# Turning the activations of an encoder trunk by VectorE squares and a trip through memory instead of by TensorE

## The chip, the cores and the metric

The kernel runs on one core of a Trainium2 chip. The metric is the device time of one execution in microseconds (us). TensorE (PE in the rows) does the matrix products; each product is a weight load (PEld) and a matmul that streams up to 512 columns past the loaded weights. ScalarE (ACT) and VectorE (DVE) prepare operands and work on results, GpSimd (POOL) does small statistics, and SyncE (SP) issues every transfer, each in the order of its queue. Each engine works through its own instructions in order.

## The reference, cut to what matters

```python
h = x                                            # (1, 256, 2048) float32
for i in range(2):
    hn = rms_norm(h, attn_norm[i])
    mix = windowed_gqa_sink(hn, ...) if i == 0 else diff_attention(hn, ...)
    h = h + mix                                  # both end in  o @ w_o  (2048 x 2048)
    gu = rms_norm(h, ffn_norm[i]) @ w_ffn_in[i]  # 2048 x 11264
    h = h + (silu(gu[..., :D_FF]) * gu[..., D_FF:]) @ w_ffn_out[i]   # 5632 x 2048
    gate = sigmoid(rms_norm(h, ple_gate_norm[i]) @ ple_w_gate[i])    # 2048 x 2048
    h = h + rms_norm(p[i] @ ple_w_proj[i], ple_post_norm[i]) * gate
```

There are 256 tokens, so every weight is read once from memory (425 MB) and used for two tiles of 128 tokens.

## The kernel before

**Products.** Every weight matrix is cut into groups (`Group`): one strip of 512 output columns, and n blocks ("k-tiles") of 128 input rows. A k-tile of the activations, transposed, is the weight operand of TensorE (`xt`, 128 inputs x 256 tokens), and the 512 columns of the weight matrix stream past it (`ws`). Both are float32 and are split in a high and a low part, so each k-tile costs three matmuls for each of the two token tiles m: x high by w high, x low by w high, x high by w low. That is six matmuls a k-tile (`Group.tile`, L176), 9600 in all.

**Weights.** SyncE loads blocks of four k-tiles into `raw` (two DMAs of 512 KB, three blocks deep, L130). `split_block` turns two k-tiles into one `ws` tile: ScalarE copies the high part (L138), VectorE subtracts it for the low part (L139). I call two k-tiles, twelve matmuls, a pair. The pool of `ws` has four tiles (`WS_BUFS`), and `Feed.next` keeps four ahead: when TensorE's program takes pair p, the split of pair p+3 is written, into the tile that pair p-1 leaves.

**Activations.** The residual `h` and the feed-forward's hidden tiles have tokens on the partitions and must be transposed to become `xt`. `Norm.turn` (L269) and `turn_hidden` (L751) do this on TensorE: eight 128x128 transposes for 512 columns (four k-tiles, two token tiles) into PSUM, then a split into `xt` on ScalarE and VectorE (L206/L207, with the norm's gain L210/L211).

**Order.** TensorE's order is the program's own. `Flow` keeps a heap of delayed pieces of work with due times in estimated us; after each matmul of a group it issues one instruction of the piece that is due, so transposes and attention are strewn between matmuls. `flow.until` forces pieces when a group needs an `xt` that isn't written yet. ScalarE, VectorE and SyncE are ordered by the framework's scheduler.

**Stages.** Attention A: qkv, scores and softmax by head, then the projection in two halves of eight k-tiles over four strips (`project`). Feed-forward: per 512 hidden columns a gate group and an up group of 16 k-tiles (`up` makes `hid`), and after 12, 12, 12 and 8 k-tiles of hidden the output groups (`PARTS`), which add to h. Then the gate of the layer embedding, 16 k-tiles by four strips. Then attention B with qkv strips, projection, and the second feed-forward. Each group that adds the last part of a strip of h calls `Norm.add` for that strip; the next matrix needs the strips in order, four k-tiles each.

Of the kernel before, what the change touches and what calls it, by code (L numbers as in the profile page):

```python
# [12 lines left out]
F32 = mybir.dt.float32  # L13
F32R = mybir.dt.float32r
# [71 lines left out]
def encoder(ctx: ExitStack, tc: tile.TileContext, x, p, attn_norm, ffn_norm, a_w_qkv, a_q_norm,  # L86
# [16 lines left out]
    tiny = pool("tiny", 4)  # L103
    mmp = pool("mmp", 4, bass.MemoryType.PSUM)
    atp = pool("atp", 4, bass.MemoryType.PSUM)

    flow = Flow()

# [33 lines left out]
    class Group:  # L142
# [30 lines left out]
        def tile(self, ps, k, m, ws):  # L173
            x, hi, lo = self.xs[k], ws[:, 0, k % 2, :], ws[:, 1, k % 2, :]
            for i, (a, w) in enumerate(((0, hi), (1, hi), (0, lo))):
                nc.tensor.matmul(ps[m], x[:, a, mslice(m)], w, start=(k == 0 and i == 0),  # L176
                                 stop=(k == self.n - 1 and i == 2))
                flow.tick(MM)

# [34 lines left out]
    def rsqrt(src, n, c, out=None):  # L214
# [10 lines left out]
        nc.gpsimd.tensor_tensor(out=r, in0=y, in1=a, op=ALU.mult)  # L225
        return r

    def gain(c):
        return gains[:, c:c + 1]

    class Stat:
# [18 lines left out]
        def col(self, m):  # L250
            return self.r[:, m:m + 1]

    class Norm:


        def __init__(self, col):
            self.col, self.stat, self.xs = col, Stat(), Slots()

        def add(self, s, delay):
            self.stat.add([h[:, m, s * W:(s + 1) * W] for m in range(NM)])  # L260
            for k in range(s * SK, (s + 1) * SK, 2):
                flow.later(delay, lambda k=k: self.turn(k))

        def turn(self, k):

            ps = at_ps()
            for j in range(2):
                for m in range(NM):
                    nc.tensor.transpose(ps[:, j, mslice(m)], h[:, m, (k + j) * P:(k + j + 1) * P], ident)  # L269
                    yield  # L270
            for j in range(2):
                xt = pair()
                split_scaled(xt[:, 0, :], xt[:, 1, :], ps[:, j, :], gain(self.col + k + j))
                self.xs.put(k + j, xt)

    class Slots:

# [79 lines left out]
                                op0=ALU.subtract, op1=ALU.add)  # L357

    phases = ExitStack()

    def phase(name):

        phases.close()
        return phases.enter_context(tc.tile_pool(name=name, bufs=1, reuse_waits="tile"))


    def qk_norm(srcs, rinv, nh, dh, dup, qp, then):
# [35 lines left out]
                yield  # L403
        split_scaled(dst[:, :, 0, :], dst[:, :, 1, :], ps, g)

    def scores(ps, q, k):

        for m in range(NM):
            for i, (a, b) in enumerate(((0, 1), (1, 0), (0, 0))):
                nc.tensor.matmul(ps[m], q[:, a, mslice(m)], k[:, b], start=(i == 0), stop=(i == 2))  # L410
                yield

    def exps(pss, d, slope, ap, extra=None):

# [42 lines left out]
    class AttentionA:  # L457
        def __init__(self, norm):
            self.norm, self.os, self.kd, self.vp = norm, Slots(), [], []
            self.ap = phase("attn0")  # L460
            self.dist = self.ap.tile([P, NM, T], F32, name="dist")

        def keys_values(self, ps):
# [74 lines left out]
        def weigh(self, j, wts):  # L538
            ps = at_ps()[:, 0, :]
            n = 0  # L540
            for e2 in range(2):
                c0 = j // 4 * P + 64 * (1 - e2)
                for kh in range(2):
                    v, wT = self.vp[kh], wts[e2]
                    for a, b in ((1, 0), (0, 1), (0, 0)):
                        nc.tensor.matmul(ps, v[:, a, c0:c0 + P], wT[:, b, kh, :], start=(n == 0), stop=(n == 11))  # L546
                        n += 1
                        yield
            busy["wT"] -= 2
            o = pair()  # L550
            split(o[:, 0, :], o[:, 1, :], ps)
            self.os.put(j, o)

        def groups(self):
            w, xs = a_w_qkv[0], self.norm.xs
# [3 lines left out]
    class AttentionB:  # L559
# [1 line left out]
            self.os, self.norm, self.hd = Slots(), norm, {}  # L561

        def start(self):
            self.ap = phase("attn1")
            self.dist = self.ap.tile([P, NM, T], F32, name="dist")
            nc.sync.dma_start(out=self.dist, in_=dist_b)

# [10 lines left out]
        def turn_side(self, hd, which, toks, b):  # L578
            s = self.hd.setdefault(hd, {"e": {}})
            t = self.ap.tile([P, 2, 2, T], F32R, name=f"qk{which}", tag=f"qk{which}", bufs=2)  # L580
            yield from to_pairs(t, toks, b * T, (gq_b, gk_b)[which])
            s[which] = t
            if which == 1:
                for c in range(2):
                    flow.later(4.5 + 2.0 * c, lambda c=c: self.scores(hd, c))

        def values(self, s):
            def done(ps):
# [9 lines left out]
        def scores(self, hd, c):  # L598
            s = self.hd[hd]
            flow.until(lambda: 0 in s and 1 in s) if not (0 in s and 1 in s) else None  # L600
            ps = at_ps()
            pss = [ps[:, m, :] for m in range(NM)]
            yield from scores(pss, s[0][:, c], s[1][:, c])
            s["e"][c] = exps(pss, self.dist, 2.0 ** (-8.0 * (hd + 1) / B_H), self.ap)
            if c == 1:
                (e1, r1), (e2, r2) = s["e"][0], s["e"][1]
                r2l = small("r2l")
                nc.vector.tensor_scalar(out=r2l, in0=r2, scalar1=nlam, scalar2=None, op0=ALU.mult)
                for m in range(NM):
                    nc.gpsimd.tensor_scalar(out=e2[:, m, :], in0=e2[:, m, :], scalar1=r2l[:, m:m + 1],  # L610
                                            scalar2=1.0, op0=ALU.mult, op1=ALU.mult)
                    nc.vector.scalar_tensor_tensor(out=e1[:, m, :], in0=e1[:, m, :], scalar=r1[:, m:m + 1],  # L612
                                                   in1=e2[:, m, :], op0=ALU.mult, op1=ALU.add)
                flow.later(9.0, lambda: self.turn(hd, e1))
# [39 lines left out]
        def out(self, hd, on):  # L654
            ps = at_ps()
            for j in range(2):
                for m in range(NM):
                    nc.tensor.transpose(ps[:, j, mslice(m)], on[m][:, j * P:(j + 1) * P], ident)  # L658
                    yield
            for j in range(2):  # L660
                o = pair()
                split_scaled(o[:, 0, :], o[:, 1, :], ps[:, j, :], subln[:, j:j + 1])
                self.os.put(2 * hd + j, o)

        def groups(self):
            w, xs, out = b_w_qkv[0], self.norm.xs, []
# [4 lines left out]
            return out  # L671


    def project(w, os, norm):

        def done(half, s):
            def add(ps):
                add_to_h(ps, s)
                if half == 1:
                    norm.add(s, 3.0)  # L680
            return add
        n = KT // 2

        class Half:
            def __len__(self):
                return max(0, len(os) - n)

            def __getitem__(self, k):
                return os[n + k]
        return [Group(w, half * n * P, n, s, (os, Half())[half], done(half, s))  # L690
                for half in range(2) for s in range(NS)]

    class FeedForward:
        def __init__(self, layer, norm):
# [1 line left out]
            self.pp, self.pstat = [], Stat()  # L696

        def start(self):
            self.fp = fp = phase(f"ffn{self.layer}")
            pt = [fp.tile([P, T], F32, name=f"pt{m}", tag=f"pt{m}", bufs=1) for m in range(NM)]  # L700
            for m in range(NM):
                nc.sync.dma_start(out=pt[m], in_=p[self.layer, 0, mslice(m), :])
            self.post = fp.tile([P, D], F32, name="post")
            nc.sync.dma_start(out=self.post, in_=ple_post_norm[self.layer:self.layer + 1, :].partition_broadcast(P)
                              .rearrange("p o d -> p (o d)"))
            self.pe = fp.tile([P, NM, D], F32, name="pe")
            flow.later(12.0, lambda: self.embedding(pt))

        def embedding(self, pt):
# [5 lines left out]
            for j in range(2):  # L715
                pp = pair()
                split(pp[:, 0, :], pp[:, 1, :], ps[:, j, :])
                self.pp.append(pp)

        def embed(self, s):  # L720
            def done(ps):
# [13 lines left out]
        def up(self, hs, k0):  # L735
            def done(ps):
                hid = []
                for m in range(NM):
# [1 line left out]
                    nc.vector.scalar_tensor_tensor(out=u, in0=ps[m], scalar=self.norm.stat.col(m), in1=self.ss[m],  # L740
                                                   op0=ALU.mult, op1=ALU.mult)
                    hid.append(u)
                for j in range(0, SK, 2):
                    flow.later(2.5, lambda j=j: self.turn_hidden(hid, j, hs, k0 + j))
            return done

        def turn_hidden(self, hid, j0, hs, k0):
            ps = at_ps()
            for j in range(2):
                for m in range(NM):  # L750
                    nc.tensor.transpose(ps[:, j, mslice(m)], hid[m][:, (j0 + j) * P:(j0 + j + 1) * P], ident)  # L751
                    yield
            for j in range(2):
                ht = pair()
                split(ht[:, 0, :], ht[:, 1, :], ps[:, j, :])
                hs.put(k0 + j, ht)

        def out(self, s, last):
            def done(ps):
                add_to_h(ps, s)  # L760
                if last:
                    self.gate.add(s, 3.0)
            return done

        def gated(self, s, nxt):
            def done(ps):
# [7 lines left out]
                    if nxt is None:  # L774
                        nc.sync.dma_start(out=out[mslice(m), c], in_=h[:, m, c])
                if nxt is not None:
                    nxt.add(s, 5.0)
            return done

        def gated_last(self, ps, m):  # L780
# [30 lines left out]

    attn_a = AttentionA(norm_a)
    norm = Norm(C_FFN)
    groups = attn_a.groups() + project(a_w_o[0], attn_a.os, norm)
    norm_b = Norm(C_ATTN + KT)
    groups += FeedForward(0, norm).groups(norm_b)
    attn = AttentionB(norm_b)
    norm = Norm(C_FFN + KT)
    groups += attn.groups() + project(b_w_o[0], attn.os, norm)
    groups += FeedForward(1, norm).groups(None)  # L820
    feed = Feed(groups)

# [85 lines left out]
```

## Time and profile before

| | |
|---|---|
| median of 3 runs | 2377.14 us (2376.62 to 2378.21) |
| the profiled execution, its own time | 2379.22 us |
| its span in the trace | 2377.4 us |
| TensorE busy | 2347.2 us, 99% of the span |
| VectorE, ScalarE busy | 57%, 47% |
| DMA engines | 52% of their time, 428.71 MB moved |

TensorE's busy time says how long something was in its pipeline, not how fast: matmuls overlap one another (a mean of 396 ns each, one started every 227 ns). What a change is worth is read from periods, from one group's start to the next.

### The profile page before, as it was taken

How to read it: one execution, taken by the hardware profiler on the slowest of the kernel's cores; microseconds unless marked ns; L12 is line 12 of the kernel's file. 1: busy time of each engine (PE TensorE's matmuls, PEld its weight loads, DVE VectorE, ACT ScalarE, POOL GpSimd, SP SyncE). 2: the span in 40 equal slices, each digit the busy share in tenths (PEclk: the TensorE clock that was granted, in tenths of full speed). 3: DMA queues.
4: the chain of work that ended last, by engine and by line, in shares of the span. 5: the costliest groups of instructions: out<-in, count | busy, mean ns of one | idle time of the engine just before them, and what ended most of it. 6: DMA issues, size and time to landing. Idle time of an engine off the chain costs nothing.

```text
span 2377.4 us, 28287 instructions
## 1 busy us (share of the span) xinstructions
PE 2347.2 (99%) x10757; PEld 1928.4 (81%) x10757; DVE 1352.4 (57%) x1604; ACT 1121.4 (47%) x1557; POOL 141.4 (6%) x311
## 2 busy tenths in 40 slices
PE   8999999999999999999999999999999999999999
PEld 6877788888888888888878888888888888888887
DVE  5777555555555454566567667655545554455564
ACT  5555454434434434455555554544444434444453
POOL 1342000000000000000110120000000000000000
PEclk9999999999999999999999999999999999999999
DMA  6433455555555555555544545555555555555554
GB/s 236 158 108 106 137 182 191 195 192 189 192 185 190 195 191 191 185 179 193 181 160 162 175 160 179 190 185 185 195 186 195 194 193 183 192 195 195 177 196 141
DMA packets 121569, 428.71 MB, mean 180 GB/s; under 512 B 13552, under 2 KB 16728, under 8 KB 121176
## 3 DMA queue, kind: packets, MB, share of 16 engines
q1 hardware_dynamic: 121432, 426.89, 51.8%
q8 instruction: 84, 1.38, 0.2%
q14 instruction: 53, 0.43, 0.1%
HBM read 424.74 MB, written 2.10 MB: 180 GB/s over the span
## 4 chain that ended last, share of the span: by engine, by line
PE 87%; DVE 1%; ACT 1%; issue 0%; POOL 0%; DVEq 0%; POOLq 0%; ACTq 0%
PE mm L176 84%; PE at L751 1%; PE at L269 1%; PE at L410 1%; PE at L635 1%; DVE ws L139 0%; ACT e L427 0%; PE at L402 0%; DVE e L612 0%; ACT v L210 0%; PE at L441 0%; ACT ws L138 0%; PE at L658 0%; DVE qk L211 0%; POOL e L610 0%
## 5 line engine op out<-in xcount | busy, mean ns | idle before, releaser
L176 PE MATMUL mm<-ws,xt 128*128 128x512 f32 x9600 | 2315.6, 396 | 6.1 <-ACT xt L206 3.9
L176 PEld LDWEIGHTS mm<-ws,xt 128*128 128x128 f32 x9600 | 1792.1, 188 | 404.9 <-ACT xt L206 4.9
L139 DVE TENSOR_TENSOR ws<-raw,ws 128x1024 fp32r<-128x1024 f32 x800 | 978.0, 1224 | 874.2 <-ACT ws L138 873.5
L138 ACT CAST ws<-raw 128x1024 fp32r<-128x1024 f32 x800 | 840.8, 1052 | 1026.8 <-PE mm L176 957.2
L217 POOL TENSOR_SCALAR rs_v<-ssum 128x2 f32<-128x2 f32 x8 | 1.5, 193 | 1707.5 <-DVE ssum L246 1707.5
L298 DVE TENSOR_TENSOR h<-mm,h 128x512 f32<-128x512 f32 x96 | 62.2, 682 | 2.3 <-PE mm L176 2.2
L210 ACT ACTIVATE xt<-at,gains 128x256 fp32r<-128x256 f32 x96 | 44.1, 474 | 32.9 <-DVE xt L211 24.2
L269 PE MATMUL at<-ident,h 128*128 128x128 f32 x192 | 52.4, 287 | 6.2 <-DMA h<-in_x_dram 6.2
L427 ACT ACTIVATE e<-e,nm 128x257 f32<-128x257 f32 (+1 forms) x96 | 48.0, 503 | 21.1 <-DVE nm L424 20.7
L206 ACT CAST xt<-at 128x256 fp32r<-128x256 f32 x108 | 37.9, 372 | 39.9 <-DVE xt L207 31.8
L211 DVE SCALAR_TENSOR_TENSOR xt<-at,gains,xt 128x256 fp32r<-128x256 f32 x96 | 44.7, 480 | 17.8 <-ACT xt L210 17.8
L207 DVE TENSOR_TENSOR xt<-at,xt 128x256 fp32r<-128x256 f32 x108 | 43.3, 418 | 14.0 <-ACT xt L206 14.0
L219 POOL TENSOR_TENSOR rs_y<-rs_v,halves 128x2 f32<-128x2 f32 (+2 forms) x29 | 49.0, 1691 | 2.4
L751 PE MATMUL at<-ident,hid 128*128 128x128 f32 x176 | 47.8, 272 | 0.0
L546 PE MATMUL at<-wT,vp 128*128 128x256 f32 x192 | 45.7, 297 | 1.3 <-DVE wT L207 1.0
L421 DVE SCALAR_TENSOR_TENSOR e<-dist,at 128x256 f32<-128x256 f32 x96 | 36.4, 413 | 10.2 <-PE at L410 9.8
L441 PE MATMUL at<-ident,e 128*128 128x128 f32 x160 | 40.6, 272 | 0.7 <-DVE e L421 0.7
L410 PE MATMUL at<-kd,qT 128*128 128x512 f32 x96 | 36.1, 400 | 3.2 <-DVE wT L207 2.5
L732 ACT ACTIVATE silu<-mm,rinv 128x512 f32<-128x512 f32 x44 | 29.9, 688 | 19.7 <-PE mm L176 19.7
L526 POOL TENSOR_SCALAR e<-e,rd 128x256 f32<-128x256 f32 x64 | 33.0, 532 | 60.4 <-DVE rd L430 60.0
L546 PEld LDWEIGHTS at<-wT,vp 128*128 128x128 f32 x192 | 33.9, 204 | 2.9 <-ACT e L427 1.1
L269 PEld LDWEIGHTS at<-ident,h 128*128 128x128 f32 x192 | 27.7, 147 | 9.4 <-DMA h<-in_x_dram 7.1
(97 smaller groups left out, 671.7 us busy)
## 6 DMA issues: line engine op xcount, KB each, us to landing
raw<-in_w_ffn_in_dram SPq DMA_DIRECT2D x352, 512.0 KB
raw<-in_w_ffn_out_dram SPq DMA_DIRECT2D x176, 512.0 KB
raw<-in_b_w_qkv_dram SPq DMA_DIRECT2D x96, 512.0 KB
raw<-in_ple_w_gate_dram SPq DMA_DIRECT2D x64, 512.0 KB
raw<-in_a_w_qkv_dram SPq DMA_DIRECT2D x40, 512.0 KB
raw<-in_a_w_o_dram SPq DMA_DIRECT2D x32, 512.0 KB
raw<-in_b_w_o_dram SPq DMA_DIRECT2D x32, 512.0 KB
raw<-in_ple_w_proj_dram SPq DMA_DIRECT2D x16, 256.0 KB
```

Source lines behind the costliest of these rows:

```text
L138: nc.scalar.copy(out=ws[:, 0], in_=src)
L139: nc.vector.tensor_tensor(out=ws[:, 1], in0=src, in1=ws[:, 0].bitcast(F32), op=ALU.subtract)
L176: nc.tensor.matmul(ps[m], x[:, a, mslice(m)], w, start=(k == 0 and i == 0), stop=(k == self.n - 1 and i == 2))
L210: nc.scalar.activation(out=hi, in_=src, func=AF.Copy, scale=scale)
L211: nc.vector.scalar_tensor_tensor(out=lo, in0=src, scalar=scale, in1=hi.bitcast(F32), op0=ALU.mult, op1=ALU.subtract)
L219: nc.gpsimd.tensor_tensor(out=y, in0=v, in1=halves[:, :n], op=ALU.pow)
L269: nc.tensor.transpose(ps[:, j, mslice(m)], h[:, m, (k + j) * P:(k + j + 1) * P], ident)
L298: nc.vector.tensor_tensor(out=hs, in0=ps[m], in1=hs, op=ALU.add)
L410: nc.tensor.matmul(ps[m], q[:, a, mslice(m)], k[:, b], start=(i == 0), stop=(i == 2))
L427: nc.scalar.activation(out=sc[:, m, :], in_=sc[:, m, :], func=AF.Exp, bias=nm[:, m:m + 1], accum_out=den[:, m:m + 1])
L546: nc.tensor.matmul(ps, v[:, a, c0:c0 + P], wT[:, b, kh, :], start=(n == 0), stop=(n == 11))
L751: nc.tensor.transpose(ps[:, j, mslice(m)], hid[m][:, (j0 + j) * P:(j0 + j + 1) * P], ident)
```

## The change

Four things change.

1. `Norm.add` and `up` no longer write TensorE transposes but call `turned`. VectorE turns the two 128x512 token tiles in 32x32 squares, with tokens of the two tiles side by side (element step two); SyncE writes the 512 KB to memory, and reads it back in four DMAs whose runs are 64 floats, so that the 128 rows of a k-tile lie on the partitions. The split into `xt` then reads SBUF. The tokens of such an `xt` alternate between the token tiles, so the weight load takes every second element (`alternate`); other `xt` keep halves (`halves_of`).
2. The tiles for the squares and the way back come from pools of the stage: `wT` in attention A, `qk0` and `qk1` in attention B, new ones in the feed-forward.
3. In attention B the six score matmuls of a map stand together, and are due 6.5 us after the keys instead of 4.5.
4. The projection of attention A is cut in parts of 8, 4 and 4 k-tiles instead of 8 and 8.

```diff
+    def halves_of(t):
+        return t.rearrange("p a (m t) -> p a m t", m=NM)
+    def alternate(t):
+        return t.rearrange("p a (t m) -> p a m t", m=NM)
...
-                nc.tensor.matmul(ps[m], x[:, a, mslice(m)], w, start=(k == 0 and i == 0),
+                nc.tensor.matmul(ps[m], x[:, a, m], w, start=(k == 0 and i == 0),
...
+    def turned(srcs, then):
+        (tag0, tag1), ap = spare[0], spare[1]
+        both = [ap.tile([P, 2, 2, T], F32R, name=t, tag=t, bufs=n).bitcast(F32).rearrange("p a b t -> p (a b t)")
+                for t, n in (tag0, tag1)]
+        st = both[0].rearrange("p (f t m) -> p f m t", m=NM, t=32)
+        for m in range(NM):
+            nc.vector.transpose(out=st[:, :, m, :], in_=srcs[m].rearrange("p (f t) -> p f t", t=32))
+        d = dram.tile([P, 2 * W], F32, name="sq32")
+        nc.sync.dma_start(out=d, in_=both[0])
+        def read():
+            for b in range(4):
+                r = slice(32 * b, 32 * b + 32)
+                nc.sync.dma_start(out=both[1][r].rearrange("f (k g i) -> f k g i", k=SK, g=4),
+                                  in_=d.rearrange("(g f) (k b i) -> b f k g i", g=4, k=SK, b=4)[b])
+            flow.later(4.0, lambda: then(both[1].rearrange("f (k t) -> f k t", k=SK)))
+        flow.later(3.0, read)
...
-        def add(self, s, delay):
-            self.stat.add([h[:, m, s * W:(s + 1) * W] for m in range(NM)])
-            for k in range(s * SK, (s + 1) * SK, 2):
-                flow.later(delay, lambda k=k: self.turn(k))
+        def add(self, s):
+            hs = [h[:, m, s * W:(s + 1) * W] for m in range(NM)]
+            self.stat.add(hs)
+            def then(xT):
+                for j in range(SK):
+                    xt, k = pair(), s * SK + j
+                    split_scaled(xt[:, 0, :], xt[:, 1, :], xT[:, j], gain(self.col + k))
+                    self.xs.put(k, alternate(xt))
+            turned(hs, then)
...
-                for j in range(0, SK, 2):
-                    flow.later(2.5, lambda j=j: self.turn_hidden(hid, j, hs, k0 + j))
+                def then(xT):
+                    for j in range(SK):
+                        ht = pair()
+                        split(ht[:, 0, :], ht[:, 1, :], xT[:, j])
+                        hs.put(k0 + j, alternate(ht))
+                turned(hid, then)
...
-                    flow.later(4.5 + 2.0 * c, lambda c=c: self.scores(hd, c))
+                    flow.later(6.5 + 2.0 * c, lambda c=c: self.scores(hd, c))
...
-    groups = attn_a.groups() + project(a_w_o[0], attn_a.os, norm)
+    groups = attn_a.groups() + project(a_w_o[0], attn_a.os, norm, (8, 4, 4))
...
-    groups += attn.groups() + project(b_w_o[0], attn.os, norm)
+    groups += attn.groups() + project(b_w_o[0], attn.os, norm, (8, 8))
```

**ScalarE, the sixth up group of the first feed-forward** (hidden columns 2560 to 3071, the last before the second round of output groups). `CAST ws<-raw` is a weight split, `CAST xt` the high part of a turned hidden tile. Before:

```order
L732 ACTIVATE silu<-mm,rinv 128x512 x2
L138 CAST ws<-raw 128x1024 x10
L206 CAST xt<-at 128x256 x3
L138 CAST ws<-raw 128x1024
L206 CAST xt<-at 128x256
L138 CAST ws<-raw 128x1024 x29
```

Of the change (one silu of the gate group stands between the previous turned tile and these rows):

```order
L207 CAST xt<-turned 128x256 x4
L777 ACTIVATE silu<-mm,rinv 128x512
L139 CAST ws<-raw 128x1024 x14
L207 CAST xt<-turned 128x256 x4
L139 CAST ws<-raw 128x1024 x27
```

The four turned tiles stand four weight splits later than the first of them stood. VectorE's rows run in the same order behind them.

**SyncE, the same place.** `raw` are weight loads, `sq` the tile in memory, `turned` the way back. Before there are weight loads alone. Of the change:

```order
L131 DMA raw<-in_w_ffn_in_dram 128x1024 x6
L131 DMA raw<-in_w_ffn_out_dram 128x1024 x8
L272 DMA sq_5251<-sq_5247 128x1024
L131 DMA raw<-in_w_ffn_out_dram 128x1024 x2
L277 DMA turned<-sq_5251 32x16x64 x4
L131 DMA raw<-in_w_ffn_out_dram 128x1024 x14
```

One block of weights stands between the way out and the way back, and the loads behind wait in the queue for both.

**SyncE, from the projection of attention B to the second feed-forward.** `pt` is the layer embedding's input, 2 x 128 KB, that TensorE transposes early in the feed-forward; `post` its gain. Before:

```order
L130 DMA raw<-in_b_w_o_dram 128x1024 x20
L702 DMA pt_12008<-in_p_dram 128x256
L702 DMA pt_12009<-in_p_dram 128x256
L704 DMA post<-in_ple_post_norm_dram 128x2048
L130 DMA raw<-in_b_w_o_dram 128x1024 x12
L130 DMA raw<-in_w_ffn_in_dram 128x1024 x16
```

Of the change:

```order
L272 DMA sq_12026<-qk_12022 128x1024
L131 DMA raw<-in_w_ffn_in_dram 128x1024 x2
L277 DMA qk_12023<-sq_12026 32x16x64 x4
L131 DMA raw<-in_w_ffn_in_dram 128x1024 x3
L747 DMA pt_12032<-in_p_dram 128x256
L747 DMA pt_12033<-in_p_dram 128x256
L749 DMA post<-in_ple_post_norm_dram 128x2048
```

The loads of `pt` move from ahead of the last twelve loads of the projection to behind the way back of the last strip and three DMAs of weights.

## Rows read from the trace of the kernel before

**Rows 1.** The page's first lines: span, busy time of TensorE
```profile
span 2377.4 us, 28287 instructions
PE 2347.2 (99%) x10757; PEld 1928.4 (81%) x10757; DVE 1352.4 (57%) x1604; ACT 1121.4 (47%) x1557; POOL 141.4 (6%) x311
```

**Rows 2.** The chain of waits, longest pieces: start us, us, what
```profile
354.32 44.48 PE mm L176 x196
...
1078.98 20.00 PE mm L176 x88
1101.74 20.00 PE mm L176 x88
```

**Rows 3.** Groups by line and shape: count | busy us, mean ns | idle before
```profile
L176 PE MATMUL mm<-ws,xt 128*128 128x512 f32 x9600 | 2315.6, 396 | 6.1 <-ACT xt L206 3.9 <-DVE xt L207 1.4 <-DVE ws L139 0.5
L176 PEld LDWEIGHTS mm<-ws,xt 128*128 128x128 f32 x9600 | 1792.1, 188 | 404.9 <-ACT xt L206 4.9 <-DVE xt L207 2.9 <-DVE ws L139 1.5
...
L298 DVE TENSOR_TENSOR h<-mm,h 128x512 f32<-128x512 f32 x96 | 62.2, 682 | 2.3 <-PE mm L176 2.2
L269 PE MATMUL at<-ident,h 128*128 128x128 f32 x192 | 52.4, 287 | 6.2 <-DMA h<-in_x_dram 6.2
L751 PE MATMUL at<-ident,hid 128*128 128x128 f32 x176 | 47.8, 272 | 0.0
```

**Rows 4.** Busy time by window, end of attention A: PE, PEld, DVE, ACT, POOL, PEclk, DMA, GB/s
```profile
248.00:268.00 20.00, 15.18 (x69) 11.71 (x69) 7.16 (x13) 6.36 (x15) 1.88 (x4) 0.83 0.33 119
252.40:258.60 6.20, 5.51 (x15) 4.45 (x16) 0.64 (x2) 0.15 (x1) 0.00 (x0) 0.50 0.89 307
```

**Rows 5.** Who waited for whom, TensorE: us in total, times, longest
```profile
PE at L410 <- DVE qk L211: 5.0, 4, 2.3
```

**Rows 6.** Windows in attention B, columns as in rows 4
```profile
1214.00:1217.00 3.00, 0.73 (x5) 0.31 (x4) 3.00 (x6) 1.39 (x2) 0.00 (x0) 1.00 0.00 0
1218.00:1221.40 3.40, 3.40 (x13) 2.82 (x12) 2.57 (x4) 0.72 (x2) 0.00 (x0) 0.51 0.81 282
1293.00:1296.00 3.00, 2.10 (x11) 1.50 (x10) 2.88 (x4) 1.03 (x2) 0.53 (x2) 1.00 0.99 315
1296.00:1299.40 3.40, 3.40 (x20) 2.95 (x20) 2.57 (x4) 0.67 (x1) 0.00 (x0) 1.00 0.21 43
```

**Rows 7.** Timeline of ScalarE and VectorE, first feed-forward: start, us, instruction, idle before
```profile
764.13 1.05 ACT L138 CAST ws<-raw 128x1024 fp32r<-128x1024 f32 x1 [0.29 <-PE mm L176]
765.08 0.37 ACT L206 CAST xt<-at 128x256 fp32r<-128x256 f32 x1
...
765.21 1.23 DVE L139 TENSOR_TENSOR ws<-raw,ws 128x1024 fp32r<-128x1024 f32 x1 [0.87 <-ACT ws L138]
766.35 0.42 DVE L207 TENSOR_TENSOR xt<-at,xt 128x256 fp32r<-128x256 f32 x1
```

**Rows 8.** Timeline where an up group ends and the next group begins
```profile
348.61 1.40 DVE L740 SCALAR_TENSOR_TENSOR hid<-mm,rinv,silu 128x512 f32<-128x512 f32 x2
348.67 2.89 PE L176 MATMUL mm<-ws,xt 128*128 128x512 f32 x12
```

**Rows 9.** A block of weights: SyncE issues, then windows, columns as in rows 4
```profile
771.93 6.20 SPq L130 DMA_DIRECT2D raw<-in_w_ffn_in_dram  x4
...
772.50:773.00 0.50, 0.50 (x4) 0.41 (x3) 0.00 (x0) 0.50 (x1) 0.00 (x0) 1.00 0.32 66
773.00:776.00 3.00, 3.00 (x15) 2.49 (x14) 1.22 (x1) 1.38 (x2) 0.00 (x0) 1.00 0.95 332
776.00:776.50 0.50, 0.50 (x4) 0.42 (x3) 0.43 (x1) 0.03 (x1) 0.00 (x0) 1.00 0.17 57
```

**Rows 10.** SyncE and TensorE at the start, loads of x in 1 KB runs; issues of two
```profile
1.17 0.93 SPq L324 DMA_DIRECT2D h<-in_x_dram  x2
3.99 2.19 PE L269 MATMUL at<-ident,h 128*128 128x128 f32 x8 [1.17 <-DMA h<-in_x_dram]
...
331.49 0.80 SPq L130 DMA_DIRECT2D raw<-in_ple_w_proj_dram  x2
```

More of the change, by code (lines that the diff above doesn't have):

```diff
@@ L105, in encoder @@
     atp = pool("atp", 4, bass.MemoryType.PSUM)
+    dram = pool("turned", 4, bass.MemoryType.DRAM)
     flow = Flow()
@@ L273, in turn @@
                 split_scaled(xt[:, 0, :], xt[:, 1, :], ps[:, j, :], gain(self.col + k + j))
-                self.xs.put(k + j, xt)
+                self.xs.put(k + j, halves_of(xt))
     class Slots:
@@ L359, in encoder, with phase @@
     phases = ExitStack()
-    def phase(name):
+    spare = [None, None]
+    def phase(name, tags):
         phases.close()
-        return phases.enter_context(tc.tile_pool(name=name, bufs=1, reuse_waits="tile"))
+        spare[:] = tags, phases.enter_context(tc.tile_pool(name=name, bufs=1, reuse_waits="tile"))
+        return spare[1]
     def qk_norm(srcs, rinv, nh, dh, dup, qp, then):
@@ L404, in to_pairs, with scores @@
         split_scaled(dst[:, :, 0, :], dst[:, :, 1, :], ps, g)
-    def scores(ps, q, k):
+    def scores(ps, q, k, together=False):
         for m in range(NM):
@@ L410, in scores @@
                 nc.tensor.matmul(ps[m], q[:, a, mslice(m)], k[:, b], start=(i == 0), stop=(i == 2))
-                yield
+                if not together:
+                    yield
+        if together:
+            yield 0.7
     def exps(pss, d, slope, ap, extra=None):
@@ L551, in weigh @@
             split(o[:, 0, :], o[:, 1, :], ps)
-            self.os.put(j, o)
+            self.os.put(j, halves_of(o))
         def groups(self):
@@ L563, in start @@
         def start(self):
-            self.ap = phase("attn1")
+            self.ap = phase("attn1", (("qk0", 2), ("qk1", 2)))
             self.dist = self.ap.tile([P, NM, T], F32, name="dist")
@@ L602, in scores @@
             pss = [ps[:, m, :] for m in range(NM)]
-            yield from scores(pss, s[0][:, c], s[1][:, c])
+            yield from scores(pss, s[0][:, c], s[1][:, c], True)
             s["e"][c] = exps(pss, self.dist, 2.0 ** (-8.0 * (hd + 1) / B_H), self.ap)
@@ L662, in out @@
                 split_scaled(o[:, 0, :], o[:, 1, :], ps[:, j, :], subln[:, j:j + 1])
-                self.os.put(2 * hd + j, o)
+                self.os.put(2 * hd + j, halves_of(o))
         def groups(self):
@@ L671, in groups, with project, __init__, __len__ @@
             return out
-    def project(w, os, norm):
-        def done(half, s):
+    def project(w, os, norm, parts):
+        class Part:
+            def __init__(self, first):
+                self.first = first
+            def __len__(self):
+                return max(0, len(os) - self.first)
+            def __getitem__(self, k):
+                return os[self.first + k]
+        def done(last, s):
             def add(ps):
                 add_to_h(ps, s)
-                if half == 1:
-                    norm.add(s, 3.0)
-            return add
[L682 to L691, printed above, removed]
+                if last:
+                    norm.add(s)
+            return add
+        out, first = [], 0
+        for n in parts:
+            out += [Group(w, first * P, n, s, Part(first), done(first + n == KT, s)) for s in range(NS)]
+            first += n
+        return out
     class FeedForward:
@@ L698, in start @@
         def start(self):
-            self.fp = fp = phase(f"ffn{self.layer}")
+            self.fp = fp = phase(f"ffn{self.layer}", (("sq32", 2), ("turned", 2)))
             pt = [fp.tile([P, T], F32, name=f"pt{m}", tag=f"pt{m}", bufs=1) for m in range(NM)]
@@ L717, in embedding @@
                 split(pp[:, 0, :], pp[:, 1, :], ps[:, j, :])
-                self.pp.append(pp)
+                self.pp.append(halves_of(pp))
         def embed(self, s):
@@ L742, in done @@
                     hid.append(u)
-                for j in range(0, SK, 2):
-                    flow.later(2.5, lambda j=j: self.turn_hidden(hid, j, hs, k0 + j))
-            return done
[L747 to L756, printed above, removed]
+                def then(xT):
[4 more added lines that the diff above has]
+                turned(hid, then)
+            return done
         def out(self, s, last):
@@ L761, in done @@
                 if last:
-                    self.gate.add(s, 3.0)
+                    self.gate.add(s)
             return done
@@ L776, in done @@
                 if nxt is not None:
-                    nxt.add(s, 5.0)
+                    nxt.add(s)
             return done
```

2 lines of the change are left out of this document (1 added, 1 removed).

## The prediction

> **What bounds the kernel now.** The page first [rows 1]: something is in TensorE's pipeline for 2347 of 2377 us, so a gain comes from taking work off TensorE or from its few waits, and a loss from new waits. Then the groups [rows 3]: 9600 of the 10757 matmuls are the weights' own. How fast these run is read from the chain of waits [rows 2], where an undisturbed piece is 196 matmuls in 44.48 us, 0.2269 us each. 9600 of them are 2179 us, and that part stays. About 200 us are transposes, attention and waits.
>
> **Transposes removed.** Their mean of 272 to 287 ns [rows 3] is latency. Their cost is in the period: between two pieces of the chain that begin alike, at 1078.98 and 1101.74, lie 22.76 us [rows 2], a group of 96 matmuls and the eight transposes strewn into it. 96 x 0.2269 are 21.79. So eight cost 0.97 us, 0.12 each: they slip in beside long matmuls. `turned` is called for 22 hidden tiles and for 20 strips of five norms (the first norm of x keeps its transposes), 42 calls of eight. Gain: 42 x 0.97 = **40.8 us**.
>
> **Projection in three parts.** At the end of attention A the second half needs heads 12 to 15 before they are done. [...] With parts of 8, 4 and 4 the k-tiles 12 to 15 are wanted 96 matmuls (22 us) later, and the strewn attention work has room. Gain: **7.9 us**. The four more groups cost eight VectorE additions of 0.68 us [rows 3], beside TensorE's work.
>
> **Scores together.** Four waits on the split keys are 5.0 us [rows 5]; after the longest (2.27 us) the clock was 0.51 for 3.4 us, 1.7 us lost, while after a wait of 0.9 us it stayed at 1.00 [rows 6]. Due 2 us later, the scores find the keys in three of four cases. [...] I take **4 us** gained, between 0 and 6.7.
>
> Gains: 40.8 + 7.9 + 4 = 52.7 us.
>
> **What the moved work waits for.** A turned tile now goes VectorE, SyncE, memory, SyncE, ScalarE, VectorE. Two delays decide, the queue and the trip.
>
> *The queue.* The split of pair p+3 needs the `ws` tile that pair p-1 leaves. Counting ScalarE's rows of the change, 12 of the 42 turned tiles stand right behind the weight split that waits for the pair just ahead of the one that needs them: hidden tiles 2, 5 and 8 of both feed-forwards, the last strip of both gates and of attention B's norm, and strips 0 to 2 after attention A. So, however early the data lands, TensorE finishes pair p-1, the weight split starts, and only then the tile's. These rows exist already: a split released by TensorE at 764.13, its tile's high part from 765.08, and VectorE's low part done at 766.77, 2.64 us on [rows 7]. TensorE can run one matmul with the high part meanwhile, so each place costs **2.5 us** (2.6 with a gain): 6 x 2.5 + 6 x 2.6 = 30.6 us. In the order before, these splits stood four weight splits earlier, and nothing waits there [rows 3]. For the other tiles the order leaves at least two pairs.
>
> *The trip.* From the end of an up group (348.67) VectorE has `hid` 1.35 us later [rows 8]. The squares: no row has such an operation. Nearest is 0.68 us for 128x512 [rows 3]; between 0 and twice that, I take 0.68 each, done at 2.7. SyncE issues in 0.4 us [rows 10]; after an issue at 771.93 a block of 1 MB begins to move some 0.6 us later and has moved by about 776.1 [rows 9], 3.6 us for 1 MB in all; the half that a pair needs takes about 1.6. The first load of x is 2.8 us from issue to use [rows 10]; its 256 KB at the same rate are 0.8, the start 0.6, and of the 1.4 left I give 0.8 to the issue and 0.6 to landing. So the write lands at 2.7 + 0.6 + 1.6 + 0.6 = 5.5. Meanwhile a block of weights (1 MB) has gone in front of the way back; it ends near 7.6. The way back is 2048 runs of 256 bytes, which no row shows: 1.6 us if like long runs, 6 at near four times that; I take 3, nearer the long runs, which are the nearest row; the factor of four is a guess that only makes the upper end. With 0.6 to land: **11.2 us** after the group's end, between 8 and 16.
>
> The output groups want hidden tile 10, the last of the part of eight k-tiles, after four k-tiles, 5.45 us: 11.2 + 0.8 for the split [rows 7] - 5.45 - 0.23 = **6.3 us** wait in each feed-forward (3.5 to 11). In parts of twelve the cover is 10.9 us and the queue's 2.5 is the larger (up to 5.3 if the trip takes 16). For norms it is 16.3 us, and the trip hides.
>
> [...]
>
> *SyncE's queue.* `pt` now stands behind the last way back and three weight DMAs, the third of which waits for a weight split that itself waits for TensorE. After attention B: the group ends, four pairs later (10.9 us) TensorE releases that split, it is done 2.4 later, and after two more issues and 0.5 MB of data ahead `pt` lands at about 16. TensorE wants it 4.4 pairs in, at 12: **4 us**. After attention A strips 2 and 3 are turned only when strips 0 and 1 have been split (two tiles each of four `wT` are taken), so SyncE gets there later still, and I take **5 us**. Both can be 0 to 6.
>
> Waits: 30.6 + 2 x 6.3 + 9 = 52.2 us.
>
> **The clock.** [...] The short waits, 2.5 us broken by one matmul, lie near the first: I let half of twelve cost 1.7 us, 10 us. The two long and two `pt` waits cost 1.7 to 3.1 each, 9 us. Together 19, between 7 and 33.
>
> VectorE gains 84 squares (57 us) at 57% load, hidden between weight splits that run three pairs ahead. The transfers add 44 MB, 10%, to engines half busy [rows 9].
>
> **The sum**, against the profiled execution's own 2379.2: - 52.7 + 52.2 + 19 = 2397.7. The median of the runs shown lies 2.1 us under that execution, so **2395.6 us**.
>
> **The rivals.**
> A. *The trip never binds* (other side): every wait is only the queue's 2.5 us and the clock holds. Sixteen waits of 2.5 are 40 us: 2379.2 - 52.7 + 40 - 2.1 = 2364 us. It decides below 48 us of waits, 3 us each. For it: a wait of 0.9 us left the clock alone [rows 6], and the DMA engines have gaps between blocks (0.17 busy from 776 to 776.5 [rows 9]). Against: the part of eight k-tiles gives only 5.45 us, and one load's issue to use alone is 2.8. Chance 0.18.
> B. *The clock holds* but the waits are as sized: 2379.2 - 52.7 + 52.2 - 2.1 = 2377 us, no change. Chance 0.15.
> C. *Short runs are slow*: a way back of 6 us puts the trip at 14 to 15. The two long waits grow by 3 each, the four under parts of twelve by about 1.5, `pt` by 2: 14 us more, about 2410. Chance 0.13.
> D. *The strided weight load slows the product.* 8256 of the 9600 matmuls now load every second element. The load is 188 ns in a cadence of 227 [rows 2, 3], so 39 ns hide; beyond, each ns costs 8.3 us, and 10 ns give 2480. No row has a strided load. [...] Chance 0.06.
>
> **How the numbers follow.** The forecast (2383 to 2408) has 0.48, A 0.18, B 0.15, C 0.13, D 0.06. What a measurement can tell from no change here is about 0.2%, 4.8 us. Faster: A, 0.18. Same: B, 0.15. Slower: the rest, 0.67. The range 2366 to 2418 leaves out D, the slow end of C and the fast half of A, 0.18. With all costs at their low ends the sum is near 2360, at their high ends near 2433.
>
> **What would show it.** Right: 336 fewer transposes; groups of TensorE's waits on `xt` from the high and the low split, 1.4 and 1.1 us, at the twelve places; a wait of 5 to 8 us before hidden tile 10 in each feed-forward; a wait for `pt` twice; no idle in the last part of projection A; clock at 0.5 behind the long waits. Wrong: a weight load over 227 ns; a period of undisturbed matmuls off 0.2269; ScalarE's first split of a turned tile waiting for a DMA at most of the twelve places (the trip is longer than I think), or no clock drop.

## The result, and the profile after

The changed kernel takes 2455.7 us (median of 4 runs, 2454.7 to 2457.98) against 2377.24 us before: 1.0331 times as long, interval 1.0313 to 1.0349. It is 78.5 us slower where 18 us were forecast. The first lines of the page and the groups that answer to [rows 1, 3]:

```profile
span 2454.3 us, 27991 instructions
PE 2378.5 (97%) x10421; PEld 1953.8 (80%) x10421; DVE 1396.6 (57%) x1696; ACT 1115.1 (45%) x1557; POOL 141.4 (6%) x311
...
L177 PE MATMUL mm<-ws,xt 128*128 128x512 f32 x9600 | 2346.0, 399 | 44.9 <-ACT xt L207 22.4 <-ACT xt L211 10.5 <-DVE xt L208 4.1
L177 PEld LDWEIGHTS mm<-ws,xt 128*128 128x128 f32 x9600 | 1852.2, 194 | 454.4 <-ACT xt L207 26.3 <-ACT xt L211 13.1 <-DVE xt L208 7.0
...
L270 DVE STREAM_TRANSPOSE sq<-hid 128x512 f32<-128x512 f32 x44 | 28.5, 687 | 0.0
```

The 336 transposes are gone (10421 matmuls instead of 10757). New idle time stands before the products, 44.9 us where 6.1 stood [rows 3]. And the mean weight load went from 188 to 194 ns. The squares take VectorE 687 ns each, the 0.68 us of the prediction.

Who waited for whom, TensorE: us in total, times, longest.

```profile
PE mm L177 <- ACT xt L207: 22.4, 10, 6.1
PE at L758 <- DMA pt<-in_p_dram: 12.5, 2, 7.0
PE mm L177 <- ACT xt L211: 10.5, 6, 2.8
...
PE mm L177 <- DVE xt L208: 4.1, 6, 0.8
PE mm L177 <- DVE xt L212: 3.7, 5, 0.7
...
PE mm L177 <- DVE ws L140: 2.1, 4, 0.5
PE mm L177 <- ACT ws L139: 1.8, 4, 0.5
```

These are 40.7 us for turned tiles and 12.5 us for `pt`, 53.2 together, where the prediction had 52.2. The 3.9 us on weight splits (`ws`) it didn't have. Hidden tile 5 of the first feed-forward, TensorE, ScalarE and VectorE:

```profile
672.38 1.04 ACT L139 CAST ws<-raw 128x1024 fp32r<-128x1024 f32 x1 [1.75 <-PE mm L177]
673.33 1.32 ACT L207 CAST xt<-turned 128x256 fp32r<-128x256 f32 x4
673.45 1.23 DVE L140 TENSOR_TENSOR ws<-raw,ws 128x1024 fp32r<-128x1024 f32 x1 [1.57 <-ACT ws L139]
...
673.78 0.50 PE L177 MATMUL mm<-ws,xt 128*128 128x512 f32 x1 [1.44 <-ACT xt L207]
674.60 1.43 DVE L208 TENSOR_TENSOR xt<-turned,xt 128x256 fp32r<-128x256 f32 x4
...
675.07 1.22 PE L177 MATMUL mm<-ws,xt 128*128 128x512 f32 x2 [0.79 <-DVE xt L208]
```

The weight split starts when TensorE ends its pair, the tile's split follows it at once (its data had landed), and TensorE waits 1.44 us, runs one matmul and waits again. From the first idle to 675.07 are 2.73 us; less one matmul's 0.23 that is 2.50 lost, the 2.5 of the prediction. The twelve places are the ones that it named: ten look like this, at two there is one wait of 2.1 or 2.8.

So the waits are as forecast, and they are not the 60 us that the forecast missed. Those show in a period. ScalarE's first activation of a gate group comes once in a gate and an up group; after and before, the same two rows:

```profile
798.96 0.69 ACT L777 ACTIVATE silu<-mm,rinv 128x512 f32<-128x512 f32 x1 [3.85 <-PE mm L177]
...
843.75 0.69 ACT L777 ACTIVATE silu<-mm,rinv 128x512 f32<-128x512 f32 x1 [3.85 <-PE mm L177]
```

```profile
779.74 1.37 ACT L732 ACTIVATE silu<-mm,rinv 128x512 f32<-128x512 f32 x2 [0.99 <-PE mm L176]
824.26 1.37 ACT L732 ACTIVATE silu<-mm,rinv 128x512 f32<-128x512 f32 x2 [0.99 <-PE mm L176]
```

Before, 44.52 us are 192 matmuls and eight transposes; without their 0.97 us 43.55 are left, 226.8 ns a matmul. After, the same 192 matmuls with no transpose, no wait and a clock of 1.00 take 44.79 us: 233.3 ns. The matmuls themselves became slower by 6.5 ns, and 8256 of them load alternating tokens: 53.7 us. The weight loads in the stretch 700 to 1000 us (min/median/max ns), before and after:

```profile
L176 PEld LDWEIGHTS mm<-ws,xt x1307: 187/188/192, 699.9 to 999.9; 128*128 128x128 f32 x187
```

```profile
L177 PEld LDWEIGHTS mm<-ws,xt x1275: 193/193/196, 699.8 to 999.9; 128*128 128x128 f32 x183
```

The trip, hidden tile 10 of the first feed-forward, from the chain of waits:

```profile
1027.79 0.68 DVE sq L270
...
1028.48 2.78 DMA sq<-sq
...
1031.28 0.57 SPq L277
...
1033.25 4.26 DMA turned<-sq
...
1037.61 0.41 ACT xt L207
...
1038.06 2.11 PE mm L177 x4
```

The up group ends at 1025.8 (VectorE starts on `hid` at 1025.84); the squares are written out from 2.7 us on, have landed at 5.4 (forecast 5.5), and the way back has landed at 11.7 (forecast 11.2). SyncE's four issues of the way back take 0.6 us each where the prediction had 0.4, and by the trace's DMA records the 2048 runs of 256 bytes move from 7.8 to 10.8 us, in the 3 us that it took. TensorE waited 6.08 us here and 6.13 in the second feed-forward (forecast 6.3).

Windows as in [rows 4]: the end of attention A, then the stretch of the way back and what follows it.

```profile
248.00:268.00 20.00, 20.00 (x111) 16.94 (x110) 13.93 (x20) 9.85 (x16) 1.87 (x4) 1.00 0.39 135
...
1030.00:1036.00 6.00, 1.98 (x9) 1.30 (x7) 2.45 (x2) 1.31 (x2) 0.00 (x0) 1.00 1.07 294
1036.00:1043.00 7.00, 4.94 (x12) 3.79 (x13) 1.43 (x4) 1.32 (x4) 0.00 (x0) 0.53 0.43 156
```

The waits at the end of attention A are gone, as is the wait on split keys [rows 5]. From 1036.4 to 1043.2 us, at the end of the long wait and behind it, the granted clock is 0.50.

### The profile page after: what moved, and what is told of

Its sections match the earlier page's. It is cut to its first block, busy times and chain, and to the rows that moved or that the text cites. A ratio compares the mean times of both kernels' runs of the same rounds, so it can differ in the third digit from the quotient of the medians.

```text
span 2454.3 us, 27991 instructions
## 1 busy us (share of the span) xinstructions
PE 2378.5 (97%) x10421; PEld 1953.8 (80%) x10421; DVE 1396.6 (57%) x1696; ACT 1115.1 (45%) x1557; POOL 141.4 (6%) x311
## 4 chain that ended last, share of the span: by engine, by line
PE 92%; DVE 2%; ACT 2%; DMA 2%; issue 1%; SPq 0%; POOL 0%; DVEq 0%; ACTq 0%
PE mm L177 88%; PE at L447 1%; ACT ws L139 1%; DVE ws L140 1%; PE at L586 1%; PE at L481 1%; PE at L675 0%; DMA pt<-in_p_dram 0%; PE at L439 0%; ACT xt L211 0%; DMA turned<-sq 0%; DVE xt L212 0%; DMA raw<-in_a_w_qkv_dram 0%; DMA sq<-sq 0%; POOL rs_y L220 0%
## 5 line engine op out<-in xcount | busy, mean ns | idle before, releaser
L177 PE MATMUL mm<-ws,xt 128*128 128x512 f32 x9600 | 2346.0, 399 | 44.9 <-ACT xt L207 22.4
L177 PEld LDWEIGHTS mm<-ws,xt 128*128 128x128 f32 x9600 | 1852.2, 194 | 454.4 <-ACT xt L207 26.3
L208 DVE TENSOR_TENSOR xt<-turned,xt 128x256 fp32r<-128x256 f32 x88 | 31.4, 420 | 36.3 <-ACT xt L207 25.5
L251 ACT ACTIVATE sq<-h 128x512 f32<-128x512 f32 x48 | 30.0, 625 | 26.6 <-DVE h L333 22.4
L428 DVE TENSOR_TENSOR qn<-mm,rr 128x512 f32<-128x512 f32 x24 | 15.8, 686 | 31.4 <-POOL rr L416 31.4
L207 ACT CAST xt<-turned 128x256 fp32r<-128x256 f32 x88 | 29.0, 401 | 9.7 <-DMA turned<-sq 9.7
L464 DVE TENSOR_REDUCE nm<-e 128x2 f32<-128x514 f32 (+1 forms) x48 | 32.3, 679 | 0.4
L785 DVE SCALAR_TENSOR_TENSOR hid<-mm,rinv,silu 128x512 f32<-128x512 f32 x44 | 30.9, 744 | 0.0
L208 DVE TENSOR_TENSOR wT<-at,wT 128x512 fp32r<-128x512 f32 x40 | 27.0, 685 | 6.7 <-ACT wT L207 6.5
```

Source lines behind the costliest of these rows:

```text
L177: nc.tensor.matmul(ps[m], x[:, a, m], w, start=(k == 0 and i == 0), stop=(k == self.n - 1 and i == 2))
L208: nc.vector.tensor_tensor(out=lo, in0=src, in1=hi.bitcast(F32), op=ALU.subtract)
```

## The experiments

**The product's weight load.** Two theories for the slower matmuls: S, the weight load of every second element; T, the traffic of the trips and squares beside TensorE. Three kernels tell them apart.

e1, the change with halves put back by the split, which reads every second element instead:

```diff
+                    x4 = halves_of(xt)
-                    split_scaled(xt[:, 0, :], xt[:, 1, :], xT[:, j], gain(self.col + k))
-                    self.xs.put(k, alternate(xt))
+                    split_scaled(x4[:, 0], x4[:, 1], xT[:, j].rearrange("p (t m) -> p m t", m=NM), gain(self.col + k))
+                    self.xs.put(k, x4)
```

(and the same for hidden tiles).

> The change with one thing taken back: the split of a turned tile reads every second element and writes the tokens in halves, so that TensorE's weight load reads 128 adjacent elements. Everything else stays: squares, trips, waits. Theory S (the step-two weight load is what costs: the period of a gate and an up group rose from 43.55, without its transposes, to 44.80 us, 6.5 ns for each of 8256 matmuls, 53.7 us): about 2402 us, the period back to 43.55, the mean weight load back to 188 ns. Rival T (the traffic of the trips or VectorE's squares slow the matmuls): about 2456 us, the period stays 44.80.

Measured: 2404.74 us, 1.0117 times the kernel before (1.0101 to 1.0132), 51 us less than the change as it was. The period is 830.35 - 786.83 = 43.52 us, that of before without its transposes:

```profile
786.83 0.69 ACT L778 ACTIVATE silu<-mm,rinv 128x512 f32<-128x512 f32 x1 [3.71 <-PE mm L177]
...
830.35 0.69 ACT L778 ACTIVATE silu<-mm,rinv 128x512 f32<-128x512 f32 x1 [3.71 <-PE mm L177]
```

The trips and squares still run, so they don't slow the matmuls. The split's strided read takes ScalarE 424 instead of 401 ns a k-tile of `hid`; the pair of waits at hidden tile 5 stays at 2.23 us (1.46 and 0.77 for 1.44 and 0.79).

e2, the kernel before with alternating tokens only (the split of `turn` and `turn_hidden` writes them; the first norm keeps halves):

```diff
-                split(ht[:, 0, :], ht[:, 1, :], ps[:, j, :])
-                hs.put(k0 + j, ht)
+                h4 = alternate(ht)
+                split(h4[:, 0], h4[:, 1], ps[:, j, :].rearrange("p (m t) -> p m t", m=NM))
+                hs.put(k0 + j, h4)
```

> The kernel before, transposes on TensorE, but the split writes the tokens of the two tiles alternating for all tiles that the change turns, so that 8256 weight loads read every second element. No trip, no squares. Theory S: 2377 + 53.7 = 2431 us, the gate and up period 44.52 + 1.25 = 45.77 us. Rival T: 2377 us, period 44.52.

Measured: 2427.38 us, 51.3 us over the runs of the kernel before beside it (2376.04), ratio 1.0214 (1.02 to 1.0228). Period 45.72 us:

```profile
792.21 1.39 ACT L741 ACTIVATE silu<-mm,rinv 128x512 f32<-128x512 f32 x2 [1.05 <-PE mm L176]
837.93 1.39 ACT L741 ACTIVATE silu<-mm,rinv 128x512 f32<-128x512 f32 x2 [1.05 <-PE mm L176]
```

e3, as e2, with the layout one step wider:

```diff
     def alternate(t):
-        return t.rearrange("p a (t m) -> p a m t", m=NM)
+        return t.rearrange("p a t -> p (a t)").rearrange("p (t a m) -> p a m t", a=2, m=NM)
```

> As the kernel before with alternating tokens, but high and low part alternate as well, so that the weight load reads every fourth element (16 bytes apart). Theory S1 (a load that isn't of adjacent elements costs the same 6.5 ns at any step): 2431 us. [...]

Measured: 2500.06 us, 1.0519 (1.0505 to 1.0534), 124 us over before. The gate and up period is 46.96 us, and the load:

```profile
801.07 1.39 ACT L741 ACTIVATE silu<-mm,rinv 128x512 f32<-128x512 f32 x2 [1.07 <-PE mm L176]
848.03 1.39 ACT L741 ACTIVATE silu<-mm,rinv 128x512 f32<-128x512 f32 x2 [1.07 <-PE mm L176]
```

```profile
L176 PEld LDWEIGHTS mm<-ws,xt x1246: 308/309/330, 699.9 to 999.8; 128*128 128x128 f32 x178
```

These periods hold eight transposes each. Without any are the pieces of 472 matmuls in the chain of waits, of the kernel before, of e2 and of e3 (start, us, what):

```profile
851.92 107.04 PE mm L176 x472
...
866.35 110.13 PE mm L176 x472
...
877.44 111.04 PE mm L176 x472
```

Theory S holds, T falls. Element step 1, 2, 4: load 188, 193, 309 ns; matmul to matmul 226.8, 233.3, 235.3 ns. Between undisturbed matmuls step four costs 8.5 ns, only 2 more than step two, though its load is 116 ns longer; that is near S1's 6.5 and not a cost that doubles with the distance, 13. The time is still far above S1's 2431 us: 8256 x 8.5 ns are 70 of the 124 us, and most of the rest lies where short matmuls stand between the products. A matmul beside a transpose takes 0.36 us in e3's chain and 0.24 in e2's, so the eight transposes of a period cost 46.96 - 192 x 0.2353 = 1.8 us instead of 0.97; and the stretch from the last gate of the first layer to the first gate of the second feed-forward, with attention B's short matmuls, is 461.0 us for 424.9, where the 8.5 ns of its 1152 strided products are 10.

**The two parts with no squares.** e4 is the kernel before with the scores' and the projection's edits word for word as in the change, and nothing else; the two calls:

```diff
-                    flow.later(4.5 + 2.0 * c, lambda c=c: self.scores(hd, c))
+                    flow.later(6.5 + 2.0 * c, lambda c=c: self.scores(hd, c))
...
-    groups = attn_a.groups() + project(a_w_o[0], attn_a.os, norm)
+    groups = attn_a.groups() + project(a_w_o[0], attn_a.os, norm, (8, 4, 4))
```

> The kernel before with only the projection of attention A in parts of 8, 4 and 4 and the scores together and 6.5 us after the keys; transposes on TensorE. By the prediction's terms: 7.9 + 4 us less, 2365 us; nothing idle from 248 to 268 us, and the waits on the split keys gone but for the longest. Rival: the gain is given back by the third part's extra additions or the scores' own loads: 2377 us.

Measured: 2360.22 us, 0.9934 (0.9921 to 0.9946), 15.8 us less than before; 11.9 were forecast. Nothing is idle at the end of attention A, and the waits on split keys are gone entirely. From the last gate of the first layer to the first gate of the second feed-forward, which holds all of attention B, the profiled execution is 7.9 us shorter (417.0 for 424.9), so the scores gave twice the 4 us of the prediction. In a row or strewn, a score matmul takes TensorE about 118 ns: six together take 0.71 us here, and in the kernel before a strewn one makes 345 to 349 ns of a step of 227.

```profile
248.00:268.00 20.00, 20.00 (x110) 17.08 (x109) 13.78 (x19) 9.10 (x16) 1.23 (x3) 1.00 0.47 160
```

**Queue or trip?** e6 is e1 with ScalarE's and VectorE's weight splits held behind the turned tile's split that the program wrote ahead of them:

```diff
     def split_block(raw, t):
...
+            while first:
+                for ins in first.pop():
+                    behind.enter_context(tc.issue_after(ins.ins))
```

> As e1, but every split of a turned tile is issued on ScalarE and VectorE ahead of the weight splits that the program writes after it, so that it no longer stands behind the one that TensorE has just released. Trips and their starts stay. Theory Q (the queue sets the waits of 2.2 us, the trip the two of 6 us): the waits at the last strips of both gates and of attention B's norm go, those of hidden tiles 5 and 8 fall to about 1 us (a trip of 11.7 us and the split against a cover of 10.9), hidden tile 10 still waits 6 to 7 us; about 2404.7 - 22 = 2383 us with some of the clock. Rival (the trip sets them all): all waits stay, 2405 us. Third possibility: ScalarE now waits for trips itself and the weight splits come late: new waits on weight splits, over 2405 us.

Measured: 2400.66 us, 1.0112 (1.0095 to 1.0128). TensorE's waits, and ScalarE's:

```profile
PE mm L181 <- ACT xt L213: 20.3, 10, 7.3
PE mm L181 <- ACT ws L143: 14.2, 10, 4.5
...
PE mm L181 <- DVE ws L144: 8.2, 18, 0.5
```

```profile
ACT xt L213 <- DMA turned<-sq: 128.6, 22, 7.5
ACT xt L217 <- DMA turned<-sq: 51.3, 10, 7.8
```

No strip of a norm is waited for any more; hidden tiles 5 and 8 cost 0.9 to 1.2 us instead of 2.2; hidden tile 10 still 6.5 and 7.3. That is theory Q. But ScalarE now waits for trips, and TensorE waits for the weight splits behind them for 22.4 us in all, where e1 has 4.9 us: the third possibility takes back most of what Q gives, and the 4.1 us that are left are less than the runs' own spread (2397.8 to 2405.5 us). The order in the change was not simply a bad one; with one queue, either the tile stands behind the weights or the weights behind the trip.

**The load of the embedding.** e7 is e1 with one number:

```diff
-            flow.later(12.0, lambda: self.embedding(pt))
+            flow.later(40.0, lambda: self.embedding(pt))
```

> As e1, with one number changed: the embedding's transposes, the first readers of its input's load, are due 40 us after the feed-forward begins instead of 12. The load's place in SyncE's queue stays. If the load is only late for that reader: the two waits of 13.1 us together go, and part of the half clock after them, 2404.7 - 13 - 6 = 2386 us. Rival: the engine waits for something else at that place and the time stays.

Measured: 2394.07 us, 1.0078 (1.0063 to 1.0093), 10.7 us less than e1. Both waits for `pt` are gone. Waits of 2.3 us that it had covered appear at two more strips (norm tiles 13.7 + 5.1 us instead of 10.6 + 3.6), so less came than forecast.

**Squares only where there is cover.** e5 takes e4's parts, e1's halves and e7's 40 us, and leaves 16 tiles to TensorE: the last hidden tile of each part, the first feed-forward's norm, and the last strip of the other norms.

```diff
-                turned(hid, then)
+                if not tight:
+                    return turned(hid, then)
+                for j in range(0, SK, 2):
+                    flow.later(2.5, lambda j=j: self.turn_hidden(hid, j, hs, k0 + j))
```

> Parts 8, 4, 4 and scores together as in e4; weight loads of adjacent elements as in e1; squares and a trip only for 26 tiles with cover (all hidden tiles but the last of each part, all strips but the last of both gates, of attention B's norm and of the second feed-forward's norm); TensorE turns the 16 others; the embedding's transposes are due 40 us after the feed-forward begins instead of 12. If the transposes are worth 0.97 us for eight and only the tiles without cover wait: 2360.2 - 26 x 0.97 = 2335 us and no waits of TensorE on a turned tile. Rival (the trips' traffic or their queue costs the feed of the weights something in any place): 2350 us or more, with waits on the weight splits or on tiles that had cover.

Measured: 2341.49 us, 0.9855 (0.984 to 0.987). No wait on a turned tile is left, but after three gate groups TensorE waits 1.2 us or more for a weight split:

```profile
PE mm L177 <- ACT ws L139: 3.2, 4, 1.5
...
PE mm L177 <- DVE ws L140: 2.1, 4, 0.5
```

Of these 5.3 us, 0.8 lie in attention A, where e4 has 1.0 as well; with the other 4.5 the sum of 2335 becomes 2339.5. e8 adds the last strips of four norms, ordered as in e6:

```diff
+                if s == NS - 1:
+                    first.append(last)
...
-                    nxt.add(s, s < NS - 1)
+                    nxt.add(s, True)
```

> As e5, with the last strips of the norms turned by squares as well (30 tiles in all, 12 left to TensorE) and the splits of these last strips issued ahead of the weight splits that the program writes after them, as in e6. Cover 16.3 us against a trip of about 12: no wait, 2335 - 4 x 0.97 = 2331 us. Rival: ScalarE, waiting there for the trip, makes weight splits late: slower than e5.

Measured: 2350.71 us, 0.9892 (0.9877 to 0.9907). The rival: TensorE's waits on the high part of a weight split grow to 9.5 us, the longest 2.9. e9 is e5 with attention B's norm given back to TensorE:

```diff
-                    nxt.add(s, s < NS - 1)
+                    nxt.add(s, False)
```

> As e5, but the strips of attention B's norm go back to TensorE's transposes as well (23 tiles by squares, 19 by TensorE). e5 shows three waits of 1.25 us or more on weight splits, each behind a gate group, where ScalarE splits the turned strip before. If the turned tiles' place in ScalarE's queue makes them: they go, 2341.5 + 3 x 0.97 - 5.3 = 2339 us. Rival (the gate's own work on ScalarE makes them): they stay, 2344 us.

Measured: 2338.84 us, 0.9838 (0.9825 to 0.9852). The waits went, and the sum is met. This is the best version: 38.5 us faster than before, 117 faster than the change. Of the 38.5 us, 15.8 are e4's, which has no squares; the 23 turned tiles give the other 22 (23 x 0.97 are 22.3).

```profile
PE mm L177 <- ACT xt L207: 0.9, 2, 0.5
...
PE mm L177 <- DVE ws L140: 0.5, 1, 0.5
```

## Why the prediction failed

**The step that failed** stands in rival D: "The load is 188 ns in a cadence of 227, so 39 ns hide; beyond, each ns costs 8.3 us." From this the sum took the strided weight load at nothing and gave its case 0.06, the author's estimate: no run had shown a strided load. The runs show neither half of the rule. A load only 5 ns longer, far under the 227, makes the period of undisturbed matmuls 6.5 ns longer (e2), and taking it back takes 51 us off the change (e1). A load 121 ns longer, 82 over the 227, makes it 8.5 ns longer (e3), where the rule gives 82. The difference between two means in a pipeline was read as free time. The edit was rated by the weight load's own duration, of which no row had a strided one; its bounds should have been put on the period, where 6.5 ns are 54 us, and kept in the range.

That step two costs nothing nearly holds for the load's own record: 193 ns (e2) against 188 for adjacent floats, and 309 at step four (e3). For the product's period it doesn't hold: 226.8, 233.3 and 235.3 ns in the kernel before, e2 and e3, which differ in the layout that the load reads. This spacing was what to weigh.

**Right, by its terms.** Transposes 42 x 0.97 = 40.8 us: e1's period is 43.52 against 44.52 us. Twelve waits behind a weight split, "1.4 and 1.1 us": they are at those twelve places, and the ten that come in two pieces, of 1.44 and 0.79 or 1.54 and 0.73 us, lose 2.5 us each. Hidden tile 10: 6.1 us for 6.3. `pt`: 12.5 us for 9; after attention B the group ended at 1574.7, the load, forecast to land 16 us later, was issued only at 1589.29, and TensorE started at 1594.71, 20 us after the group.

**Right in kind, off in size.** Projection and scores gave 15.8 us (e4) for 11.9. The projection's 7.9 are the 4.8 us idle from 248 to 268 and half of the 6.2 us at a granted clock of 0.50 [rows 4]; the scores' 4 was the author's estimate, which no run shows. e4 has 7.9 us in the stretch with attention B, the scores, and so about 8 in the projection.

**The clock** came out near its 19 us (7 to 33). Its 10 us for the short waits, six at 1.7, come from the one wait of 2.27 us, behind which the clock was 0.51 for 3.4 us [rows 6]; the 3.1 at the top for each long one is half of 6.2 us at 0.50 [rows 4]. No row showed what follows a wait broken by one matmul. In eleven stretches of the change the granted clock is 0.50 or 0.51: seven of 3.4 us, three of 6.8 and one of 13.7. Their windows add up to (total us, then busy us):

```profile
sum 58.04, PE 45.86 PEld 35.97 DVE 16.01 ACT 9.11 POOL 0.43; mean PE 4.17 PEld 3.27 DVE 1.46 ACT 0.83 POOL 0.04
```

Half of TensorE's 45.9 us, 22.9, is what a clock of 0.50 cost it, an estimate; 1.7 of that is in a stretch at 169 us that the kernel before has as well, so the change added about 21. The same count closes the sum of e1 against e4, which differ by the squares alone and by 44.5 us. The transposes are -40.8. TensorE's waits on tiles, weight splits and `pt` are 59.7 in e1 and 2.1 in e4, so +57.6. The low clock cost, by the same estimate, 24.7 in e1 and 1.4 in e4, +23.3. In ten split waits the one matmul between has a record of 0.50 us where 0.23 are work, +2.7. That is 42.8 of 44.5 (waits and clock are those of the profiled executions, which are 47.3 apart). The rule of halves for the short waits was fair: of twelve in the change seven are followed by a granted clock of 0.50 or 0.51, and behind the same pair of waits (1.44 and 0.79 us) it was 0.51 from 674.6 to 678.0 at hidden tile 5 of the first feed-forward, but 1.00 at tiles 2 (466 to 470) and 8 (880 to 884).

With e1's 51 us added, the forecast of 2395.6 would have been 2447. The clock's 2 more, 3.7 more of the forecast waits (53.2 and 2.7 against 52.2; the ten matmuls count here too), and the 3.9 on weight splits, less the 3.9 that e4 gave beyond the forecast, make it about 2452, against 2455.7. The rest isn't assigned.

**Not settled.** Why step two lengthens the period by 6.5 ns when the load's own time grows by 5, and step four by only 2 more when it grows by another 116, isn't shown: in e3 the load of 309 ns is longer than the period of 235.3, so the records of loads overlap one another, and what of a load a matmul must wait for can't be read from them. Steps above four, and a strided matmul operand, were not tried.

## What to carry to other kernels

Rate an edit to an operand that TensorE loads by the period from matmul to matmul, not by whether the load is shorter than the period; thousands of matmuls turn 6 ns into more than the whole change was worth (8256 x 6.5 ns are 53.7 us, its gains were put at 52.7). Where a layout has to be undone, let the engine with room do it: here ScalarE's strided read cost 23 ns a k-tile (e1), TensorE's strided load 6.5 ns in each matmul (e2). And a detour through memory paid where there was more cover than the trip takes and the tile didn't share a queue with work that is released just in time (e9: 22 us for 23 tiles); elsewhere TensorE's own 0.97 us for eight transposes is cheaper than the waits of 2 to 7 us seen here.

## What the hardware showed that was not expected

Element step 2 in the weight load costs 6.5 ns a matmul with the load's record only 5 ns longer; step 4 makes the record 309 ns and the spacing of undisturbed matmuls 235.3, but a matmul beside a transpose then takes 0.36 us where it took 0.24. Runs of 256 bytes, at 246 and 194 GB/s where the weight loads behind them had 389, were far from the four times as slow that the prediction guessed at most. Windows in the trip of hidden tile 10, while the way back moved (GB/s last), and behind it; then the packets of the first of them:

```profile
1034.00:1035.00 1.00, 0.00 (x0) 0.00 (x0) 0.32 (x1) 0.00 (x0) 0.00 (x0) 1.00 1.25 246
1035.00:1036.00 1.00, 0.00 (x0) 0.00 (x0) 0.00 (x0) 0.00 (x0) 0.00 (x0) 1.00 1.29 194
...
1037.00:1038.00 1.00, 0.00 (x0) 0.00 (x0) 0.00 (x0) 0.39 (x2) 0.00 (x0) 0.50 0.98 389
```

```profile
DMA packets 994, 0.25 MB, mean 246 GB/s; under 512 B 994, under 2 KB 994, under 8 KB 994
```

In the first two windows all but two of the packets are under 512 bytes, so it is the way back alone that moves there, at half to two thirds of the rate of the weight loads behind it.
